# Two banded attention layers of a four-layer network: gates applied when the output is read back, projections spread over more units, modulation weights moved ahead of the output weights

## The chip, the cores and the metric

One core of a Trainium2 chip runs the whole network, 49,595 instructions in one launch. The metric is device time in microseconds (us). The kernel before was timed three times: 3087.85, 3089.04 and 3092.97 us, median 3089.04. Its engines are TensorE (PE, with its weight loads PEld), VectorE (DVE), ScalarE (ACT), GpSimd (POOL) and SyncE (SP), whose queue issues nearly all DMAs.

## The reference, cut to what matters

Four layers, each `x = x + gate * rmsnorm(mixer(h), g_post)` with `h = rmsnorm(x, g_pre) * (1 + scale) + shift`, on 1024 latent and 256 context tokens of width 1024, in float32. Scale, shift and gate are the modulation, `silu(c) @ w_ada + b_ada` with a 1024x3072 matrix for each layer. The mixers are banded attention (layers 0 and 3), latent attention (layer 1) and a chunked recurrence (layer 2). The change is in the banded layers:

```python
q_l, k_l, v_l, z_l = jnp.split(h_lat @ w_in, cuts, axis=-1)     # 1024, 256, 256 and 1024 columns
q_l = apply_rope(q_l.reshape(bsz, n_lat, A_HEADS, A_HEAD_DIM), cos, sin)   # 16 heads of 64, 4 key heads
p = sink_softmax(jnp.where(mask, logits, NEG_INF), sink_l)      # own block, its two neighbours, 256 ctx keys
o_l = jnp.moveaxis(o, 0, 1).reshape(bsz, n_lat, A_WIDTH)
y_l = (o_l * jax.nn.silu(z_l)) @ w_out
```

Layer 0 also makes queries, gates and outputs of the context tokens; layer 3 makes them for the latent tokens alone.

## The kernel before, in words

Every product is done in three matmuls, on numbers split into a high and a low part (high x high, high x low, low x high). Weights come in pieces of 512 KB: `add_chunk` and `add_mod` put pieces into one list (`todo`), `fetch` (L136) loads them in that order into three buffers (`raw`), and `step` (L151) takes the first loaded piece: a weight is split by one engine (high part) and another (low part), a modulation chunk of 256 columns, two pieces, is multiplied on PE at once (`mod_piece`, L356, and `flush_mod`, L374). `need(chunk)` steps until that chunk is there, and so also handles all that stands ahead of it in the list. `plan` (L623) sets the order of the list. In it, the next layer's twelve modulation chunks stood behind `z` chunks 2 to 7 (one each), and the other six behind the first six of the eight pieces of the output weights `wo`. Layer 3 has no next layer and no modulation.

`layer_a` (L681) first makes keys and values, then works through *units*: (key head g, tile t of 128 queries), 40 in layer 0 (two context tiles, then eight latent ones, for each g) and 32 in layer 3. Step s of the loop runs `stage_s(s)` (scores, maximum, exponential, normalization) and `stage_pv(s-1)` (transposes, `ph`/`pl` split, product with the values). PE has spare time in both, and into it `fill(n)` draws n steps of the generator `projections`, one matmul a step, which makes the queries `q` of group g (written out to `qd`) and the gates `z` (written out to `zd` with silu applied). The counts drawn are in `fs` (behind each of the four heads) and `fp` (behind each key block). Where something isn't made in time, `made_for` draws until it is. A unit before needed its queries two units ahead (`load_q`) and its two gate blocks in `stage_pv` (`load_z`, L849), where POOL multiplied the output by them (L938) ahead of the write to `od`.

At s = `last` the rest of the projections is drawn, the buffers of the projection weights and of the layer's input are given up, and `wo` takes their place: eight pieces, dealt out over the remaining units by `pacer`. At s = nu - `early` (39 of 40 in layer 0, 29 of 32 in layer 3) `boundary` (L505) begins and its matmuls become the filler. For each tile it loads the output of all heads (`go`, 512 KB, one buffer), splits it into `gh` and `gl` in halves of 512 columns (`halves`, L586), multiplies by `wo` in 48 matmuls of 512 columns, and adds the normed result to x; in layer 0 it also norms the tile for the next layer. The split of the next tile is called behind the fourth of a tile's eight rounds.

Query weights `wq` and gate weights `wz` have one buffer each, so a chunk can only be split once the chunk before it of the same kind is used up. Before, q and z pieces took turns so that one kind's split lay beside the other's matmuls.

The order written in the program isn't that of the queues: the whole program is laid out once, by a planner with a clock of its own, which can place a later instruction ahead of earlier ones of its engine when by its clock those are not yet ready. On the chip each queue then runs in the planned order.

Of the kernel before, what the change touches and what calls it, by code (L numbers as in the profile page):

```python
# [9 lines left out]
F32 = mybir.dt.float32  # L10
# [3 lines left out]
ALU = mybir.AluOpType  # L14
# [14 lines left out]
PIECES = ((0, 512), (512, 512), (1024, 256))  # L29
# [21 lines left out]
class Dit:  # L51
# [543 lines left out]

    def gload_T(self, od):

        def load(t, wk):
            o = wk.tile([128, 8, 128], F32, name="go", bufs=1)
            self.nc.sync.dma_start(out=o, in_=od[:, t * 128:t * 128 + 128].rearrange("(k p) t -> p k t", p=128))  # L600
            return o

        def split(o, wk):
            return self.halves(wk, lambda h: o[:, 4 * h:4 * h + 4, :], "act", "pool")
        return load, split
# [18 lines left out]
    def plan(self, i):  # L624
# [4 lines left out]
        P = {}  # L629
# [5 lines left out]
        if kind == "a":  # L635
            P["kv"] = self.add_chunk(w_in, 1024, 512, eo=256)
            if i == 0:
                mods(8, 12, 0)
            for g in range(4):
                P["q", g] = self.add_chunk(w_in, g * 256, 256, eo=256)  # L640
                for x in (2 * g, 2 * g + 1):
                    P["z", x] = self.add_chunk(w_in, 1536 + 128 * x, 128)
                    if x >= 2:
                        mods(x, x + 1)
            P["wo"] = [self.add_chunk(ins[f"l{i}_w_out"][x * 512:(x + 1) * 512, :], 0, 1024, 4) for x in range(2)]
            wos = [self.todo.pop() for _ in range(8)][::-1]
            rest = [x for x in list(range(4 // 2)) + list(range(8, 12))]
            for x in range(8):
                self.todo.append(wos[x])
                for m in rest[:1]:  # L650
                    mods(m, m + 1)
                rest = rest[1:]
            for m in rest:
                mods(m, m + 1)
        elif kind == "b":
# [25 lines left out]
    def layer_a(self, i, hpool, hT, hs):  # L681
# [96 lines left out]
        def proj_q(g, pieces):  # L778

            w = P["q", g]  # L780
            for t0, m in pieces:
                for b in range(2):
                    for ps in piece(w, slice(128 * b, 128 * b + 128), t0, m):
                        yield
                    if b == 0:
                        e = self.eo_even(qp, ps, t0, m)
                    else:
                        self.eo_odd(qp, e, ps, t0, m, lambda p: qd[g][p])
                made.add(("q", g, t0))

        def proj_z(x, pieces):

            w = P["z", x]
            for t0, m in pieces:
# [6 lines left out]
                nc.sync.dma_start(out=zd[x * 128:(x + 1) * 128, t0:t0 + m], in_=zs[:, 0:m])  # L801
                made.add(("z", x, t0))

        def projections():

            ctx = [PIECES[2]] if need_ctx else []
            for g in range(4):
                yield from proj_q(g, ctx + [PIECES[0]])
                yield from proj_z(2 * g, ctx + list(PIECES[:2]))
                self.need(P["z", 2 * g + 1])  # L810
                yield from proj_q(g, [PIECES[1]])
                if g < 3:
                    self.need(P["q", g + 1])
                yield from proj_z(2 * g + 1, ctx + list(PIECES[:2]))
                if g < 3:
                    self.need(P["z", 2 * g + 2])

        pq = projections()

        def made_for(kind, xs, t):  # L820

            for x in xs:
                while (kind, x, t * 128 // 512 * 512) not in made:
                    next(pq)


        fs, fp = (5, 5, 5, 2), (2, 2, 2, 2, 1)
        units = [(g, t) for g in range(4) for t in qtiles]
# [11 lines left out]
        def load_q(u):  # L840
            g, t = units[u]
            made_for("q", (g,), t)
            q = p2.tile([128, 2, 4, 128], F32R, name="qT", bufs=2)
# [4 lines left out]
            st[u] = {"qT": q}  # L848

        def load_z(u):  # L850
            g, t = units[u]
            made_for("z", (2 * g, 2 * g + 1), t)
            z = p2.tile([128, 2, 128], F32, name="zin", bufs=2)
            nc.sync.dma_start(out=z, in_=zd[g * 256:(g + 1) * 256, t * 128:(t + 1) * 128]
                              .rearrange("(a p) t -> p a t", p=128))
            st[u]["z"] = z

# [48 lines left out]
        def stage_pv(u, fill, end=False):  # L906
            g, t = units[u]
            pr, kbs = st[u]["pr"], st[u]["kbs"]
            load_z(u)
            v2 = grp[g][1]  # L910
# [25 lines left out]
            for b in range(2):  # L936
                nc.vector.tensor_tensor(out=o[64 * b:64 * b + 64], in0=pv_[:, b], in1=uv[:, b], op=ALU.add)  # L937
            nc.gpsimd.tensor_tensor(out=o, in0=o, in1=st[u]["z"], op=ALU.mult)  # L938
            nc.sync.dma_start(out=od[g * 256:(g + 1) * 256, t * 128:(t + 1) * 128]
                              .rearrange("(a p) t -> p a t", p=128), in_=o)  # L940
            del st[u]

        load_group(0)
        made_for("q", (0,), qtiles[-1])
        made_for("z", (0,), qtiles[-1])
        load_q(0)
# [10 lines left out]
        early = 3 if i == self.depth - 1 else 1  # L957
        last = nu - 7
        for s in range(nu + 1):
# [20 lines left out]
            if s == nu - early:  # L980
                for w in wo:
                    self.need(w, FAST)
                bg = self.boundary(i, wo, [gq, wop], self.gload_T(od), gq, 1 if i == self.depth - 1 else 0)
                next(bg)
# [1025 lines left out]
```

## Time and profile before

| | us |
|---|---|
| median of three runs | 3089.04 |
| the profiled execution | 3097.26 |
| its span on the core | 3095.5 |
| TensorE matmul busy in the span | 2861.1 (92%) |
| VectorE / ScalarE / GpSimd busy | 1727.5 / 1261.0 / 1288.7 |

By stretches of the span: layer 0 has its units from about 200 to 707 us, its boundary overlapping from 677 on to about 820; layer 3 has its units from about 2600 to 3040 and its boundary from 2978 to the end. A busy PE counts also the time in which it works at the lower clock, so the granted clock is read beside it.

### The profile page before, as it was taken

Reading aid. Unit: us, or ns where it says so; the run is one execution under the profiler, and the core shown is the slowest. Engines: PE = TensorE matmul, PEld = TensorE weight load, DVE = VectorE, ACT = ScalarE, POOL = GpSimd, SP = SyncE. Lnnn points to the kernel's source line nnn. Section 1 sums busy time; section 2 is a strip of 40 time slices with the busy share of each in tenths; the row PEclk is TensorE's granted clock in tenths of the full one; section 3 lists DMA queues with packets and bytes.
Section 4 is the critical chain, followed back from the end, with each engine's and each line's share of the span. In section 5 each row is a group of like instructions: output and inputs, shape, how many; then the busy total and the mean of one; then the engine's idle time right before and its main releaser. Section 6 shows DMA issues by size and latency. Waiting matters only on the chain.

```text
span 3095.5 us, 49595 instructions
## 1 busy us (share of the span) xinstructions
PE 2861.1 (92%) x17344; PEld 2478.1 (80%) x17344; DVE 1727.5 (56%) x3807; ACT 1261.0 (41%) x2665; POOL 1288.7 (42%) x1535
## 2 busy tenths in 40 slices
PE   6799999989999999999899999998887999999898
PEld 4678888768877788888787789998776788888777
DVE  3337667665522366666456644245387744666772
ACT  2226556453312355555433323132264422555552
POOL 2445555545653010100353331236475445555552
PEclk9899999999999999999999899999898999999999
DMA  7453544554354311111343343699585545434433
GB/s 236 142 151 100 176 145 125 177 159 144 97 162 160 104 44 33 34 39 31 115 144 117 123 155 121 196 310 287 199 254 201 193 130 166 123 111 137 143 91 114
DMA packets 455259, 439.85 MB, mean 142 GB/s; under 512 B 38658, under 2 KB 389146, under 8 KB 455010
## 3 DMA queue, kind: packets, MB, share of 16 engines
q1 hardware_dynamic: 448832, 426.55, 43.8%
q10 hardware_dynamic: 5746, 9.48, 1.0%
q8 instruction: 138, 2.26, 0.3%
q0 software_dynamic: 432, 0.66, 0.1%
q14 instruction: 111, 0.91, 0.1%
HBM read 301.68 MB, written 135.53 MB: 141 GB/s over the span
## 4 chain that ended last, share of the span: by engine, by line
PE 54%; DVE 11%; DMA 8%; issue 4%; ACT 3%; POOL 3%; SPq 1%; ACTq 0%; POOLq 0%; DVEq 0%
PE n L73 30%; PE w L73 18%; PE n L76 5%; DVE acc L1407 1%; DMA e<-rmd 1%; DMA raw<-in_l_w_in_dram 1%; DVE mx L1257 1%; ACT ph L81 1%; DVE cl L90 1%; POOL hl L90 1%; DVE pl L90 1%; DMA qpd<-eo_t 1%; DMA gdd<-e 1%; DVE big L426 1%; DMA raw<-in_l_w_out_dram 1%
## 5 line engine op out<-in xcount | busy, mean ns | idle before, releaser
L90 DVE TENSOR_TENSOR pl<-n,ph 128x512 fp32r<-128x512 f32 x488 | 330.0, 686 | 114.6 <-ACT ph L81 97.1
L81 ACT ACTIVATE ph<-n 128x512 fp32r<-128x512 f32 x488 | 284.4, 597 | 224.9 <-PE n L76 171.8
L73 PE MATMUL n<-ph,v 128*128 128x256 f32 (+1 forms) x992 | 292.3, 337 | 19.1 <-ACT ph L81 13.5
L76 PE MATMUL n<-ident,p 128*128 128x128 f32 x1952 | 292.6, 277 | 8.9 <-DVE o L937 3.1
L73 PE MATMUL n<-wh,hh 128*128 128x256 f32 x960 | 278.2, 290 | 15.6 <-DVE sg L1738 12.6
L895 ACT ACTIVATE p<-p,nm 128x641 f32<-128x641 f32 (+2 forms) x288 | 221.0, 769 | 155.5 <-DVE nm L893 122.0
L73 PE MATMUL n<-wl,hh 128*128 128x256 f32 x960 | 275.1, 287 | 0.0
L73 PE MATMUL n<-wh,hl 128*128 128x256 f32 x960 | 274.9, 286 | 0.0
L76 PEld LDWEIGHTS n<-ident,p 128*128 128x128 f32 x1952 | 236.6, 143 | 43.9 <-ACT p L1260 4.2
L902 POOL TENSOR_SCALAR p<-p,rl 128x640 f32<-128x640 f32 (+2 forms) x288 | 213.8, 754 | 129.2 <-DVE rl L900 95.0
L891 DVE CUSTOM_DVE_ANT_0 p<-w,mask 128x640 f32<-128x640 f32 (+2 forms) x288 | 208.2, 745 | 100.1 <-PE w L73 67.3
L73 PE MATMUL n<-pl,v 128*128 128x512 f32 (+1 forms) x656 | 237.6, 362 | 17.8 <-DVE pl L90 17.3
L1311 POOL TENSOR_TENSOR o<-o,z 128x256 f32<-128x256 f32 x40 | 30.4, 760 | 440.6 <-ACT o L1310 266.0
L73 PE MATMUL w<-ks,qT 128*128 128x256 f32 (+1 forms) x1088 | 199.5, 309 | 12.0 <-DVE mx L891 7.0
L73 PEld LDWEIGHTS n<-ph,v 128*128 128x128 f32 x992 | 175.5, 190 | 37.3 <-ACT ph L81 21.7
L73 PEld LDWEIGHTS n<-wh,hh 128*128 128x128 f32 x960 | 187.7, 196 | 19.5 <-DVE sg L1738 14.1
L73 PEld LDWEIGHTS w<-ks,qT 128*128 128x128 f32 x1088 | 176.4, 190 | 30.6 <-DVE mx L891 12.3
L73 PEld LDWEIGHTS n<-wl,hh 128*128 128x128 f32 x960 | 187.7, 196 | 0.1
L73 PEld LDWEIGHTS n<-wh,hl 128*128 128x128 f32 x960 | 187.5, 195 | 0.0
L90 POOL TENSOR_TENSOR wl<-raw,wh 128x1024 fp32r<-128x1024 f32 x38 | 96.7, 2550 | 162.7 <-DVE wh L83 161.0
L73 PEld LDWEIGHTS n<-pl,v 128*128 128x128 f32 x656 | 125.0, 191 | 35.2 <-DVE pl L90 29.4
L73 PE MATMUL n<-hh,wh 128*128 128x512 f32 (+1 forms) x336 | 125.4, 373 | 6.2 <-DVE eo_t L276 5.7
(349 smaller groups left out, 7557.1 us busy)
## 6 DMA issues: line engine op xcount, KB each, us to landing
raw<-in_l_w_ada_dram SPq DMA_DIRECT2D x96, 512.0 KB
raw<-in_l_w_in_dram SPq DMA_DIRECT2D x72, 512.0 KB
qT<-qd SPq DMA_DIRECT2D x576, 64.0 KB
raw<-in_l_w_out_dram SPq DMA_DIRECT2D x32, 512.0 KB
vd<-v SPq DMA_DIRECT2D x60, 256.0 KB
xd<-xt SPq DMA_DIRECT2D x30, 512.0 KB
od<-o SPq DMA_DIRECT2D x112, 128.0 KB
go<-od SPq DMA_DIRECT2D x28, 512.0 KB
```

The source lines that it names most:

```text
L73: self.nc.tensor.matmul(out, lhsT, rhs, start=start, stop=stop)
L76: self.nc.tensor.transpose(out, in_, self.ident)
L81: nc.scalar.activation(out=out, in_=in_, func=AF.Copy)
L90: e.tensor_tensor(out=lo, in0=src, in1=as32(hi), op=ALU.subtract)
L426: nc.vector.tensor_scalar(out=h32[:, kk, :], in0=ps[:, k * 128:(k + 1) * 128], scalar1=self.mod[i][:, 8 + kk, v:v + 1], scalar2=self.mod[i ...
L891: nc.vector.tensor_tensor_reduce(out=p[:, 0:n], in0=ps[:, s0:768], in1=mask[:, mo:mo + n], scale=1.0, scalar=-3.0e38, op0=ALU.add, op1=ALU ...
L895: nc.scalar.activation(out=p[:, 0:n + 1], in_=p[:, 0:n + 1], func=AF.Exp, scale=0.125, bias=nm[:, j:j + 1], accum_out=lsum[:, j:j + 1])
L902: nc.gpsimd.tensor_scalar(out=pr[y][:, 0:n], in0=pr[y][:, 0:n], scalar1=rl[:, y:y + 1], scalar2=0.5, op0=ALU.mult, op1=ALU.mult)
L1257: nc.vector.tensor_reduce(out=mx[:, 1:2], in_=pl, op=ALU.max, axis=AX.X)
L1311: nc.gpsimd.tensor_tensor(out=o, in0=o, in1=z, op=ALU.mult)
L1407: nc.vector.scalar_tensor_tensor(out=a, in0=xp[:, t0 + o + j:t0 + o + j + n], scalar=cw[:, j, b:b + 1], in1=a, op0=ALU.mult, op1=ALU.add)
```

## The change

In `plan`, the modulation chunks stand between the q and z chunks, one behind each from `z0` on and three behind `z6`; none stands among the output weights. The chunks of q and z change places.

```diff
-            for g in range(4):
-                P["q", g] = self.add_chunk(w_in, g * 256, 256, eo=256)
-                for x in (2 * g, 2 * g + 1):
+            for n, (kd_, x) in enumerate((("q", 0), ("z", 0), ("q", 1), ("z", 1), ("q", 2), ("z", 2), ("z", 3), ("q", 3), ("z", 4),
+                                          ("z", 5), ("z", 6), ("z", 7))):
+                if kd_ == "q":
+                    P["q", x] = self.add_chunk(w_in, x * 256, 256, eo=256)
+                else:
                     P["z", x] = self.add_chunk(w_in, 1536 + 128 * x, 128)
-                    if x >= 2:
-                        mods(x, x + 1)
+                if 0 < n < 11:
+                    mods(n - 1, n if n < 10 else 12)
...
-            for x in range(8):
-                self.todo.append(wos[x])
-                for m in rest[:1]:
-                    mods(m, m + 1)
```

The generator makes all of q0 first and runs the gates one group behind the queries; the last two gate blocks come one behind the other. More steps are drawn for each unit in layer 0, one fewer in layer 3, and `last` is later.

```diff
+            yield from proj_q(0, ctx + lat)
+            self.need(P["q", 1])
+            for g in range(1, 4):
+                yield from proj_q(g, ctx + lat[:1])
+                yield from proj_z(2 * g - 2, ctx + lat)
+                self.need(P["z", 2 * g - 1])
+                yield from proj_q(g, lat[1:])
                 if g < 3:
                     self.need(P["q", g + 1])
+                yield from proj_z(2 * g - 1, ctx + lat)
+                self.need(P["z", 2 * g])
+            yield from proj_z(6, ctx + lat)
+            self.need(P["z", 7])
+            yield from proj_z(7, ctx + lat)
...
-        fs, fp = (5, 5, 5, 2), (2, 2, 2, 2, 1)
+        fs, fp = ((6, 6, 5, 2), (2, 2, 2, 2, 2)) if need_ctx else ((5, 5, 4, 2), (2, 2, 2, 2, 1))
...
-        last = nu - 7
+        last = nu - (5 if need_ctx else 6)
```

The units no longer load or apply their gates; `boundary` loads them beside the output, one tile at a time, and POOL multiplies 1024 columns ahead of the split.

```diff
-            nc.gpsimd.tensor_tensor(out=o, in0=o, in1=st[u]["z"], op=ALU.mult)
...
+            for a, n in ((od, "go"), (zd, "gz"))[:1 if zd is None else 2]:
+                x.append(wk.tile([128, 8, 128], F32, name=n, bufs=1))
+                self.nc.sync.dma_start(out=x[-1], in_=a[:, t * 128:t * 128 + 128].rearrange("(k p) t -> p k t", p=128))
...
+            if len(x) > 1:
+                self.nc.gpsimd.tensor_tensor(out=o, in0=o, in1=x[1], op=ALU.mult)
```

## Rows read from the trace of the kernel before

**Rows 1.** The page, part 1: busy time of each engine over the span.

```profile
PE 2861.1 (92%) x17344; PEld 2478.1 (80%) x17344; DVE 1727.5 (56%) x3807; ACT 1261.0 (41%) x2665; POOL 1288.7 (42%) x1535
```

**Rows 2.** Busy time by stretch: its length, engines' busy us, PE clock, DMA share, GB/s.

```profile
200.00:250.00 50.00, 41.87 (x249) 36.07 (x249) 33.37 (x93) 24.19 (x59) 28.05 (x40) 0.97 0.43 133
250.00:590.00 340.00, 336.44 (x2023) 288.44 (x2022) 233.76 (x632) 193.45 (x418) 188.99 (x302) 1.00 0.45 136
590.00:690.00 100.00, 79.39 (x508) 61.27 (x507) 66.79 (x171) 49.02 (x99) 50.01 (x71) 0.93 0.62 194
690.00:797.00 107.00, 107.00 (x513) 89.15 (x512) 57.45 (x100) 41.62 (x67) 53.53 (x62) 1.00 0.39 131
2600.00:2640.00 40.00, 38.72 (x210) 33.04 (x209) 30.32 (x72) 19.94 (x44) 27.52 (x31) 1.00 0.44 132
2640.00:2905.00 265.00, 257.30 (x1408) 218.82 (x1407) 184.39 (x451) 148.52 (x304) 150.75 (x216) 0.99 0.42 123
2905.00:2980.00 75.00, 57.13 (x301) 47.19 (x300) 59.12 (x138) 41.56 (x87) 44.52 (x64) 0.84 0.48 138
2978.00:3088.00 110.00, 108.89 (x526) 90.42 (x524) 44.26 (x83) 39.51 (x77) 37.37 (x53) 1.00 0.32 106
```

**Rows 3.** Waits of PE, 590 to 690 us: releaser, us in total, times, longest.

```profile
PE n L73 <- DMA raw<-in_l_w_ada_dram: 9.2, 4, 4.8
PE n L73 <- ACT ph L81: 5.0, 3, 3.4
PE n L73 <- DVE pl L90: 4.4, 2, 2.3
PE w L73 <- DMA qT<-qd: 1.3, 2, 1.0
```

**Rows 4.** PE's groups of the modulation, 590 to 690 us: busy us, mean ns, idle before.

```profile
L73 PE MATMUL n<-raw,cs 128*32 128x256 f32 x112 | 10.1, 458 | 9.2 <-DMA raw<-in_l_w_ada_dram 9.2
L73 PE MATMUL n<-sel,part 128*128 128x2 f32 x32 | 5.1, 259 | 0.0
```

**Rows 5.** The same two groups of PE, 250 to 590 us.

```profile
L73 PE MATMUL n<-raw,cs 128*32 128x256 f32 x80 | 5.4, 385 | 0.0
L73 PE MATMUL n<-sel,part 128*128 128x2 f32 x16 | 2.1, 236 | 0.0
```

**Rows 6.** Waits of PE, 2905 to 2980 us.

```profile
PE n L73 <- DVE pl L90: 5.4, 4, 2.6
PE n L73 <- ACT ph L81: 4.7, 2, 3.9
PE w L73 <- DVE mx L891: 4.6, 5, 2.4
```

**Rows 7.** Waits of PE, 200 to 250 us.

```profile
PE w L73 <- DMA qT<-qd: 3.6, 1, 3.6
```

**Rows 8.** POOL's groups over the span, gate product and a two-input product of 1024 columns.

```profile
L90 POOL TENSOR_TENSOR wl<-raw,wh 128x1024 fp32r<-128x1024 f32 x38 | 96.7, 2550 | 162.7 <-DVE wh L83 161.0 <-DMA q<-qd 1.0 <-DVE mod L385 0.6
L938 POOL TENSOR_TENSOR o<-o,zin 128x256 f32<-128x256 f32 x72 | 55.2, 767 | 120.2 <-DVE o L937 108.8 <-DMA qT<-qd 5.0 <-issue 2.7
```

**Rows 9.** Timeline of one boundary tile of layer 3: start us, us, engine, instruction.

```profile
3056.03 0.37 SPq L600 DMA_DIRECT2D go<-od  x1
...
3060.16 0.63 ACT L81 ACTIVATE gh<-go 128x512 fp32r<-128x512 f32 x1 [3.33 <-DMA go<-od]
...
3060.87 1.29 POOL L90 TENSOR_TENSOR gl<-go,gh 128x512 fp32r<-128x512 f32 x1 [3.14 <-ACT gh L81]
...
3065.07 0.62 PE L73 MATMUL w<-wo0h,gh 128*128 128x512 f32 x2
...
3066.91 0.37 SPq L600 DMA_DIRECT2D go<-od  x1
```

**Rows 10.** Timelines of POOL and DVE, one moment ahead of layer 3's boundary.

```profile
2935.11 3.30 POOL L90 TENSOR_TENSOR wo1l<-raw,wo1h 128x1024 fp32r<-128x1024 f32 x1
...
2936.13 2.29 DVE L893 SCALAR_TENSOR_TENSOR nm<-mx,nsink 128x1 f32<-128x1 f32 x1
```

More of the change, by code (lines that the diff above doesn't have):

```diff
@@ L594, in halves, with gload_T, split @@
         return gh, gl
-    def gload_T(self, od):
+    def gload_T(self, od, zd=None):
         def load(t, wk):
[L599 to L603, printed above, removed]
+            x = []
+            for a, n in ((od, "go"), (zd, "gz"))[:1 if zd is None else 2]:
+                x.append(wk.tile([128, 8, 128], F32, name=n, bufs=1))
+                self.nc.sync.dma_start(out=x[-1], in_=a[:, t * 128:t * 128 + 128].rearrange("(k p) t -> p k t", p=128))
+            return x
+        def split(x, wk):
+            o = x[0]
+            if len(x) > 1:
+                self.nc.gpsimd.tensor_tensor(out=o, in0=o, in1=x[1], op=ALU.mult)
             return self.halves(wk, lambda h: o[:, 4 * h:4 * h + 4, :], "act", "pool")
@@ L788, in proj_q @@
                         self.eo_odd(qp, e, ps, t0, m, lambda p: qd[g][p])
-                made.add(("q", g, t0))
+                made.add((g, t0))
         def proj_z(x, pieces):
@@ L801, in proj_z, with made_for @@
                 nc.sync.dma_start(out=zd[x * 128:(x + 1) * 128, t0:t0 + m], in_=zs[:, 0:m])
-                made.add(("z", x, t0))
         def projections():
             ctx = [PIECES[2]] if need_ctx else []
[L807 to L811, printed above, removed]
+            lat = list(PIECES[:2])
+            yield from proj_q(0, ctx + lat)
[5 more added lines that the diff above has]
+                yield from proj_q(g, lat[1:])
                 if g < 3:
                     self.need(P["q", g + 1])
-                yield from proj_z(2 * g + 1, ctx + list(PIECES[:2]))
-                if g < 3:
-                    self.need(P["z", 2 * g + 2])
-        pq = projections()
[L820 to L824, printed above, removed]
-        fs, fp = (5, 5, 5, 2), (2, 2, 2, 2, 1)
+                yield from proj_z(2 * g - 1, ctx + lat)
[3 more added lines that the diff above has]
+            yield from proj_z(7, ctx + lat)
+        pq = projections()
+        def made_for(g, t):
+            while (g, t * 128 // 512 * 512) not in made:
+                next(pq)
+        fs, fp = ((6, 6, 5, 2), (2, 2, 2, 2, 2)) if need_ctx else ((5, 5, 4, 2), (2, 2, 2, 2, 1))
         units = [(g, t) for g in range(4) for t in qtiles]
@@ L841, in load_q @@
             g, t = units[u]
-            made_for("q", (g,), t)
+            made_for(g, t)
             q = p2.tile([128, 2, 4, 128], F32R, name="qT", bufs=2)
@@ L848, in load_q @@
             st[u] = {"qT": q}
[L850 to L856, printed above, removed]
         def cols(t):
@@ L908, in stage_pv @@
             pr, kbs = st[u]["pr"], st[u]["kbs"]
-            load_z(u)
             v2 = grp[g][1]
@@ L943, in layer_a @@
         load_group(0)
-        made_for("q", (0,), qtiles[-1])
-        made_for("z", (0,), qtiles[-1])
+        made_for(0, qtiles[-1])
         load_q(0)
@@ L982, in layer_a @@
                     self.need(w, FAST)
-                bg = self.boundary(i, wo, [gq, wop], self.gload_T(od), gq, 1 if i == self.depth - 1 else 0)
+                bg = self.boundary(i, wo, [gq, wop], self.gload_T(od, zd), gq, 1 if i == self.depth - 1 else 0)
                 next(bg)
```

5 lines of the change are left out of this document (removed).

## Prediction, made before the changed kernel was run

> **What bounds the kernel now.** I read the busy time of the engines first: TensorE works for 2861.1 of 3095.5 us and the next engine, VectorE, for 1727.5 [rows 1]. The matmuls are the same before and after, so only time in which TensorE stands still, or runs at its lower clock, can be won or lost. Second, the busy time by stretch, to see where that time lies in the two layers that the change touches [rows 2]. While projections fill the units, PE stands still for 3.6 of 340 us in layer 0 (250 to 590) and 7.7 of 265 us in layer 3 (2640 to 2905), at a clock of 1.00 and 0.99. Where the filler has run out, it stands still for 20.6 of 100 us (590 to 690, clock 0.93) and 17.9 of 75 us (2905 to 2980, clock 0.84). The beginnings lose 8.1 of 50 us in layer 0 and 1.3 of 40 us in layer 3. The boundaries lose nothing and 1.1 us. So some 39 us of idle PE and the slow clock in two stretches are what this change can reach. Third, the waits of PE in those stretches, to see what ends them: in layer 0 the largest is the load of modulation weights, 9.2 us in four waits, then the split of the probabilities (5.0 and 4.4 us) [rows 3]. In layer 3, which has no modulation, all of it is VectorE and ScalarE being late with the units' own work, 5.4, 4.7 and 4.6 us [rows 6].
>
> **The change part by part.** I sum against the profiled execution, 3097.3 us; it is 8.2 us over the median of the runs shown, and the difference found is carried to that median.
>
> *Modulation away from the output weights (layer 0).* Beside `wo`, 590 to 690 us, stand 112 matmul rows of modulation, 16 to a chunk, so seven chunks: 10.1 + 5.1 = 15.2 us of PE, 2.2 us a chunk, and 9.2 us of waiting for their weights [rows 4]. In the filled stretch five chunks (80 rows) took 5.4 + 2.1 = 7.5 us, 1.5 us a chunk, with no wait at all [rows 5]. Six of the seven move into filled units. That takes away the 9.2 us of waits and 6 x 0.7 = 4 us of slow work: 13 us. The cover at the new place is the projections and units that PE has to do meanwhile.
>
> *Two more filled units in layer 0, one in layer 3.* By the counts in the code a unit of five key blocks draws 19 + 10 = 29 steps instead of 26 in layer 0, 16 + 9 = 25 instead of 26 in layer 3. Of 1152 steps in layer 0, 217 stood ahead of the first unit and 145 do now; 22 were left over for unit 33, now 64 for unit 35. In layer 3 (768 steps) nothing was left, and now 37 are, at unit 26. The work is moved, not saved: the win is what a unit loses without filler. In layer 0 that is the waits on the splits and on queries, 5.0 + 4.4 + 1.3 = 10.7 us over the six units from 33 on [rows 3], 1.8 us each, so 3.6 us for two. In layer 3 it is 17.9 us over four units, 4.5 each, and the clock: of 57.1 busy us at 0.84 some 9 us, 2.3 a unit [rows 2]. At most 6.8 us are won there.
>
> *What is late next in layer 3.* The eight pieces of `wo` must still be split between the last projection and the boundary, now in three units' time instead of four, on the engines that PE already waits for. So I count half of the 6.8, 3 us; the ends are nothing and 6.8. In layer 0 the eight pieces lie in fewer units too, but without twelve modulation pieces between them; I take 1 us lost, between nothing and the 9.4 us of both split waits.
>
> *New waits for weights.* Queries and gates no longer take turns everywhere. q1's weights can be split only behind q0's last matmul, and q1 is the first filler now, where z1 was. The same holds for z6 and z7, each needed right behind the gate block before it, and in layer 0 three modulation chunks and z7, seven pieces of 512 KB through three buffers, are called for together. Queued behind such a wait on PE are the units' scores; the planner can put units ahead of it, and the queue of SP can load early. The trace has no such wait in a filled stretch. Below, the price is nothing, as for the five chunks in rows 5; above, it is the same 9.2 us of modulation loads once more [rows 3] and, at each layer's start, a second wait like the 3.6 us for queries [rows 7]: 16 us in all. A loss only, since nothing is taken off PE here. I take 4 us in layer 0, 2 at the start of layer 3.
>
> *Gates in the boundary.* POOL gives up 72 products of 0.77 us and gets 18, of ten and eight tiles, of the size of a two-input product that takes 2.55 us [rows 8]: 55 us go, 46 come, none of it on PE. SP loses 72 loads and gets 18. What counts is the chain of a tile in layer 3 [rows 9]: the load is issued at 3056.03, the high split starts at 3060.16 and the low one ends at 3062.16; the tile's matmuls begin at 3065.07. With 2.55 us put between load and split, the high part ends at 3060.16 + 2.55 + 0.63 = 3063.3 and the low part at 3064.7, both ahead of the matmuls. So it is hidden, with 1.7 us over for the high part and about 1.3 us for the low one, which is used behind two pairs of matmuls (0.62 us a pair, overlapping). The gates' load goes behind the output's on the same queue. If it lands within 1.3 us of it, or is issued earlier (its buffer comes free earlier), nothing is lost; if it takes a second 4.13 us, 2.9 us are lost in each tile. The DMA engines are at 0.32 and 0.39 there [rows 2], so I stay near the lower end: 1 us, between nothing and 18 x 2.9 = 52 us.
>
> Where POOL's products cost something is VectorE: the tiny 128x1 `nm` of a unit, took 2.29 us from 2936.13 and ended at 2938.42, and POOL's two-input product, begun before it, ended at 2938.41 [rows 10]. In layer 3 six tiles or so (62 us of units beside the boundary, 2978 to 3040, by 10.9 us a tile [rows 9]) will have the 2.55 us product beside units that still run, so VectorE may be held for up to 6 x 2.55 = 15 us. PE has boundary matmuls to do then, so I add nothing. The Trainium skill, "SBUF — State Buffer", section "Who interferes with whom", says that the two engines share a pair of ports as a lock: an instruction of VectorE with two inputs in that memory stands still until GpSimd's is through. The trace agrees in that row. By the rule the hold comes with every product that meets an `nm`, so I leave it 0.02 of the slower side.
>
> **The sum.** Layer 0: -13 - 3.6 + 1 + 4 = -11.6. Layer 3: -3 + 2 = -1. Boundaries +1. Together -11.6, of which I take -11: 3097.3 - 11 = 3086.3 in a profile like this one, 3089.0 - 11 = 3078 us for the median.
>
> **The rivals.**
>
> *The waits travel along.* The modulation loads are late again where three chunks and z7 come together (9.2 us), and both starts lose 3.6 us: -11.6 + (9.2 + 7.2 - 6) = -1, so 3088 us. For it: single buffers, and a queue that can't leave its planned order when a load takes longer than planned. Against: five chunks in filled units without a wait.
>
> *The boundary is gated by its loads: slower.* Output and gates, 1 MB a tile, land one after the other, and the product and the splits run late, 2.9 us in each of 18 tiles, at worst +52. It decides once the second load lands more than 1.3 us behind the first. At half of it, 1.5 us a tile, the sum is -11 + 26 = +15, so 3104 us. For it: one buffer each, and the next load is issued only when the tile's last low split is done (3066.91, behind 3065.59 + its duration). Against: DMA engines two thirds idle, and the gates' buffer is free 4 us before the output's.
>
> *All of the tail is filled.* PE loses nothing from the split waits or the clock either: layer 0's 20.6 us of idle and some 6 of clock, half of layer 3's 27: about -27 + 4 waits for weights, so 3066 us. Against: 64 and 37 steps are drawn in a lump and not dealt out, and three or four units in each layer still have no filler.
>
> *The planner undoes it.* Since it can pull later work forward already, fewer forced draws may leave its order as good as it was: 0, 3089 us. It shares its place with the first rival.
>
> **How the numbers follow.** A change of less than 0.2%, 6.2 us, can't be told from none here. The forecast, -6 to -18, gets 0.46; the full tail, -18 to -30, 0.14; the waits that travel and the planner, between -6 and +6, 0.26; the boundary, or a start that costs more than both tails give, over +6, 0.12, with the 0.02 for held units 0.14. So faster 0.60, same 0.26, slower 0.14. The range goes from the full tail, 3063, to the upper part of no change, 3094; outside are the gated boundary and the last of the tail, 0.18.
>
> **What would show it.** Right: 590 to 690 without a wait for the modulation load; PE idle in layer 0's last units cut from 20.6 to near 10 us and the clock near 1.00; layer 3 idle for about 15 us ahead of its boundary; the boundary's PE as full as before, with the product ending some 2 us ahead of the tile's first matmul. Wrong: waits of PE for modulation or for `wz` near the last gate blocks, more than 12 us of idle at the start of layer 0, or gaps on PE ahead of each boundary tile with the gates' load as the releaser.

## The result, and the profile after

The changed kernel takes 3107.2 us (median of four runs, 3106.71 to 3107.87), where the kernel before took 3088.8 beside it: 1.0057 times as long, 95% interval 1.004 to 1.0075. It is 18 us slower. The forecast was 3078 us, 3063 to 3094, and slower had 0.14.

The profiled execution of the changed kernel is 3106.71 us, at its median; that of the kernel before was 8 us above its own. So the two profiles differ by 9.4 us only, and a stage read from one pair of them is good to some microseconds. First the page's first part, to be held against [rows 1]:

```profile
PE 2860.1 (92%) x17344; PEld 2472.4 (80%) x17344; DVE 1737.2 (56%) x3807; ACT 1261.6 (41%) x2665; POOL 1288.0 (41%) x1481
```

The work is as large as before, and POOL has its 54 instructions less. Next the stretches that answer to those of [rows 2]: 682 to 821 us is layer 0's boundary, and layer 3's tail is read 9 us later, as it begins later here (length, then busy us of PE, PEld, DVE, ACT, POOL, PE's clock, DMA share, GB/s):

```profile
250.00:590.00 340.00, 331.34 (x2021) 281.43 (x2021) 231.65 (x630) 189.50 (x409) 161.18 (x263) 0.99 0.44 132
590.00:690.00 100.00, 80.50 (x446) 65.02 (x445) 62.74 (x148) 43.73 (x90) 52.15 (x63) 0.88 0.52 159
682.00:821.00 139.00, 130.28 (x605) 105.93 (x603) 68.58 (x117) 48.99 (x82) 81.20 (x76) 0.98 0.41 129
2640.00:2905.00 265.00, 258.71 (x1427) 219.86 (x1426) 184.71 (x462) 150.04 (x306) 136.63 (x199) 1.00 0.38 112
2914.00:2989.00 75.00, 62.62 (x317) 51.25 (x317) 55.61 (x125) 38.02 (x79) 44.47 (x56) 0.91 0.53 153
```

PE stands still for 8.7 us in layer 0's filled units (before 3.6), for 19.5 us between 590 and 690 at a clock of 0.88 (before 20.6 at 0.93), and for 8.7 us in a boundary in which [rows 2] show none up to 797 us. Only layer 3's tail has gained: 12.4 us still, at 0.91 (before 17.9 at 0.84).

To place the time I cut each profile at the same events: from the first matmul of layer 0's query projection to the first `wo` matmul ("units 0"), from there to the first projection of layer 1 ("boundary 0"), from there to the first query projection of layer 3 ("layers 1, 2"), and to layer 3's first `wo` matmul ("units 3"). What follows, layer 3's boundary up to the last write of the output, is 95 us in every kernel below. Each ratio is to runs of the kernel before from the same round; their median is 3088.8 to 3091.8 us, so medians of different rounds can be compared to some 3 us only. Labels with a_ start from the changed kernel, those with b_ from the one before, those with due_ from b_mods_gates_due.

| kernel | median us | ratio to before, 95% interval | units 0 | boundary 0 | layers 1, 2 | units 3 |
|---|---|---|---|---|---|---|
| before | 3088.8 | 1 | 522.0 | 126.5 | 1762.6 | 429.9 |
| after | 3107.2 | 1.0057 (1.004 to 1.0075) | 528.5 | 138.7 | 1762.4 | 422.9 |
| a_mods_even | 3101.4 | 1.0033 (1.002 to 1.0046) | 527.7 | 135.5 | 1771.5 | 425.6 |
| a_nogate | 3085.0 | 0.9972 (0.996 to 0.9984) | 522.8 | 127.1 | 1762.7 | 421.1 |
| a_dve | 3108.2 | 1.0052 (1.0032 to 1.0071) | 529.1 | 135.1 | 1761.3 | 424.9 |
| b_gates | 3108.7 | 1.0053 (1.0038 to 1.0068) | 531.7 | 137.0 | 1761.9 | 424.0 |
| b_mods | 3068.2 | 0.9922 (0.99 to 0.9944) | 501.2 | 127.1 | 1752.6 | 427.1 |
| b_mods_gates | 3094.3 | 1.0008 (0.9994 to 1.0022) | 512.0 | 138.9 | 1763.8 | 424.7 |
| b_mods_gates_due | 3078.1 | 0.9963 (0.995 to 0.9976) | 502.0 | 141.0 | 1752.8 | 423.0 |
| b_mods_gates_two | 3090.1 | 1.0004 (0.9994 to 1.0013) | 510.4 | 135.2 | 1766.3 | 426.1 |
| due_load_only | 3068.8 | 0.9928 (0.9913 to 0.9943) | 503.9 | 127.1 | 1759.4 | 427.3 |
| due_product_only | 3090.8 | 1.0003 (0.9992 to 1.0014) | 505.3 | 133.8 | 1776.5 | 424.7 |
| due_two_dve | 3084.9 | 0.9983 (0.9969 to 0.9996) | 508.1 | 132.2 | 1755.4 | 430.1 |
| b_mods_g3 | 3070.0 | 0.9927 (0.991 to 0.9945) | 502.0 | 127.1 | 1758.1 | 425.6 |
| b_mods_counts | 3080.7 | 0.9972 (0.9957 to 0.9986) | 513.1 | 126.7 | 1758.2 | 425.1 |
| b_mods_last | 3077.5 | 0.9963 (0.9949 to 0.9976) | 501.0 | 128.8 | 1764.4 | 428.6 |
| b_mods_draws | 3075.6 | 0.9955 (0.994 to 0.9969) | 507.2 | 127.5 | 1758.4 | 421.9 |

So after lost 6.5 us in units 0 and 12.2 in boundary 0, and won 7.0 in units 3. In units 0 as a whole PE stands still as long as before (32.7 us, before 32.3): the loss is longer busy time, at a granted clock of 0.96 instead of 0.98. In boundary 0, 6.6 of the 12.2 us are idle time (8.7 us, before 2.1), the rest busy time (clock 0.98, before 1.00).

Layers 1 and 2 have the same source in all but three of them (due_product_only, and the two kernels with two buffers, see below), but not the same planned order, and their length lies between 1752.6 and 1771.5 us in the profiles of the others: no verdict below rests on that column. One execution is also not the median. The profiled one of a_mods_even is 13 us above its kernel's median; those of the others are within 6 us of theirs, but for that of the kernel before.

What PE waits for in the changed kernel, 600 to 700 us (releaser, us in total, times, longest):

```profile
PE n L73 <- DVE pl L90: 7.4, 2, 4.1
PE n L73 <- DMA raw<-in_l_w_ada_dram: 6.3, 2, 5.9
PE n L73 <- ACT ph L81: 1.5, 2, 1.2
PE n L73 <- DVE wzh L83: 1.3, 1, 1.3
```

and in its boundary, 690 to 820 us:

```profile
PE w L73 <- POOL gl L90: 6.4, 4, 2.1
PE w L73 <- ACT gh L81: 0.9, 1, 0.9
```

Of the three signs named for "wrong", the first is there: PE waits for a modulation load, as in [rows 3], now at the batch of three chunks, and for `wz` behind it. The second isn't: from 154 to 250 us PE is still for 4.6 us, not over 12. The third is half there: gaps ahead of the boundary's matmuls, but the releaser is the low split behind the product and not the gates' load.

### The profile page after: what moved, and what is told of

It reads as the page before. It is cut to its first block, busy times and chain, and to the rows that moved or that the text cites. A ratio compares the mean times of both kernels' runs of the same rounds, so it can differ in the third digit from the quotient of the medians.

```text
span 3104.9 us, 49425 instructions
## 1 busy us (share of the span) xinstructions
PE 2860.1 (92%) x17344; PEld 2472.4 (80%) x17344; DVE 1737.2 (56%) x3807; ACT 1261.6 (41%) x2665; POOL 1288.0 (41%) x1481
## 5 line engine op out<-in xcount | busy, mean ns | idle before, releaser
L73 PEld LDWEIGHTS n<-wh,hh 128*128 128x128 f32 x960 | 187.1, 195 | 20.6 <-DVE sg L1728 14.5
## 6 DMA issues: line engine op xcount, KB each, us to landing
raw<-in_l_w_ada_dram SPq DMA_DIRECT2D x96, 512.0 KB
raw<-in_l_w_in_dram SPq DMA_DIRECT2D x72, 512.0 KB
raw<-in_l_w_out_dram SPq DMA_DIRECT2D x32, 512.0 KB
xd<-xt SPq DMA_DIRECT2D x30, 512.0 KB
go<-od SPq DMA_DIRECT2D x28, 512.0 KB
```

The costliest lines, as they stand in the source:

```text
L73: self.nc.tensor.matmul(out, lhsT, rhs, start=start, stop=stop)
```

## The experiments

**The batch of three modulation chunks.** In the changed kernel, chunks are dealt out so that none stands right ahead of `z7`.

```diff
-                if 0 < n < 11:
-                    mods(n - 1, n if n < 10 else 12)
+                mods(*((0, 0), (0, 1), (1, 2), (2, 3), (3, 5), (5, 6), (6, 7), (7, 9), (9, 10), (10, 12), (0, 0), (0, 0))[n])
```

> The changed kernel with the three modulation chunks behind z6 moved up to z2, q3 and z5, so that none stands between z6 and z7. Theory: the loss in layer 0's units is the wait of TensorE for modulation weights where three chunks are called together; then the stretch around 600 to 615 us has no such wait, the units end 8 to 10 us sooner and the time is 3097 to 3100 us. Rival: it is the dealing itself (64 steps in a lump, the output weights split in fewer units); then the wait goes, another takes its place and the time stays at 3107 us within 3.

It gave 3101.4 us, between the two; its interval and that of after just overlap. The load wait has gone, but units 0 are 527.7 us in its profile, 0.8 less than in the changed kernel. Waits of PE, 600 to 700 us:

```profile
PE n L73 <- DVE pl L90: 8.1, 3, 4.0
PE w L73 <- DVE mx L883: 2.3, 2, 2.1
PE n L73 <- ACT ph L81: 1.6, 1, 1.6
```

So this wait was real, but not the main cause: the units' own splits stand behind it and take its place. What taking it away is worth, between nothing and the 6 us of the medians, stays open, since the profiled execution is 13 us above its median.

**The gates in the boundary, from both sides.** a_nogate is the changed kernel without the gates' load and product (its result is without the gates):

```diff
-                bg = self.boundary(i, wo, [gq, wop], self.gload_T(od, zd), gq, 1 if i == self.depth - 1 else 0)
+                bg = self.boundary(i, wo, [gq, wop], self.gload_T(od), gq, 1 if i == self.depth - 1 else 0)
```

> The changed kernel without the gates in the boundary: neither loaded nor multiplied, so the gates are left out of the result. Theory: the load and the product in the chain of each tile cost layer 0's boundary its 12 us; then that boundary is 116 to 117 us long as before, layer 3's stays, and the time is 3094 to 3097 us. Rival: the boundary is late for what came before it (output weights, the next layer's weights); then it stays near 128 us and the time near 3107 us.

It takes 3085.0 us, 22 less than after (26 by the ratios), more than the theory gave; boundary 0 is back at 127.1, 11.6 us shorter, and units 0 are 5.7 shorter. With the gates left out, the rest of the change is 0.28% faster than the kernel before, some 9 us.

b_gates is the kernel before with the gates moved and nothing else:

```diff
-    def gload_T(self, od):
+    def gload_T(self, od, zd=None):
...
-            load_z(u)
...
-            nc.gpsimd.tensor_tensor(out=o, in0=o, in1=st[u]["z"], op=ALU.mult)
```

> The kernel before with this part alone: gates multiplied in the boundary, none in the units; list, generator and counts as before. Theory: it loses the 12 us of the boundary and wins little in the units (72 loads and products fewer, some 2 us): 3097 to 3101 us. Rival: the product only hurts beside the later tail; then 3087 to 3090 us.

It takes 3108.7 us, as slow as the whole change: both theories had too little. Boundary 0 grows by 10.5 us, and units 0 by 9.7, which neither foresaw. The modulation loads, still beside `wo` here, are later than before (in total, times, longest, 560 to 700 us; [rows 3] has 9.2):

```profile
PE n L73 <- DMA raw<-in_l_w_ada_dram: 15.9, 3, 8.7
```

**The modulation alone.** The kernel before, with all twelve chunks behind the gate chunks and none beside `wo`:

```diff
-                    if x >= 2:
-                        mods(x, x + 1)
+                    mods(*((0, 1), (1, 2), (2, 4), (4, 5), (5, 7), (7, 8), (8, 10), (10, 12))[x])
...
-            wos = [self.todo.pop() for _ in range(8)][::-1]
...
```

> The kernel before with this part alone: the six modulation chunks that stood among the output weights stand behind z chunks, one or two at each, none among the output weights. Theory: as predicted for this part, waits of 9.2 us and some 4 us of slow work go: 3076 to 3081 us. Rival: the waits only move to other places, since the tail's time is set by the splits of the output weights: 3086 to 3090 us.

3068.2 us, 24 less than before beside it (3091.8), and better than the theory. It is the fastest kernel run. Busy times of the kernel before from 154 to 250 us, then of b_mods from 154 to 250, 250 to 570 and 570 to 670 us, and below them the waits of PE in b_mods from 560 to 680:

```profile
154.00:250.00 96.00, 86.49 (x467) 74.47 (x468) 42.30 (x107) 29.26 (x69) 48.14 (x53) 0.94 0.50 147
```

```profile
154.00:250.00 96.00, 95.45 (x558) 82.38 (x558) 46.24 (x126) 33.30 (x79) 52.57 (x62) 0.97 0.59 174
250.00:570.00 320.00, 316.96 (x1949) 269.76 (x1948) 216.99 (x596) 179.55 (x390) 176.34 (x276) 1.00 0.49 145
570.00:670.00 100.00, 87.22 (x501) 72.17 (x501) 74.04 (x186) 57.09 (x119) 61.24 (x88) 0.95 0.52 163
```

```profile
PE n L73 <- ACT ph L81: 6.8, 4, 2.3
PE n L73 <- DVE pl L90: 3.3, 2, 2.2
PE w L73 <- DVE mx L881: 2.3, 2, 1.5
```

No load is left among the waits (9.2 us before), and in the start, 154 to 250 us, PE stands still for 0.6 us, before for 9.5. Over the whole of units 0 it stands still for 16.1 us instead of 32.3, and its busy time is 4.6 us shorter: together the 20.8 us that units 0 are shorter. The split waits are as large as in [rows 3].

**Gates on top of it.** b_mods_gates joins the two.

> The kernel before with two parts: modulation among the z chunks and gates multiplied in the boundary of both layers; order, counts and last unit as before. Theory: the parts add up, modulation alone gave -24 us and gates alone +17 us, so 3083 to 3088 us, with layer 0's boundary 137 us long, and what the changed kernel lacks against this one, some 20 us, is due to the new order of the projections and its counts. Rival: the two parts get in each other's way and this is as slow as the changed kernel, 3100 to 3108 us; then order and counts cost nothing.

3094.3 us: the gates cost 26 us on this base, eleven in units 0 and twelve in boundary 0, and eat the whole gain. Both theories placed it wrongly, the median in between. Busy times, 250 to 570 us, to be held against the second line above:

```profile
250.00:570.00 320.00, 312.04 (x1917) 264.07 (x1915) 224.68 (x616) 185.78 (x404) 154.22 (x259) 1.00 0.43 129
```

PE is still for 8.0 us in the filled units, not 3.0. The code says why this could be: `load_z` also *drew* the gate projections. Without its demand the draws that it forced (30, 40 and 40 steps, counted in the code) are left for the lump at s = `last`, 132 steps instead of 22.

b_mods_gates_due puts the demand back without the load:

```diff
             pr, kbs = st[u]["pr"], st[u]["kbs"]
+            made_for("z", (2 * g, 2 * g + 1), t)
```

> Modulation among the z chunks and gates in the boundary, with order and counts of before, and z still drawn when a unit of before would have needed it (the draw alone, no load). Theory: taking the gates out of the units took away the draws that kept the projections in time (30, 40 and 40 steps in layer 0), so that 132 steps instead of 22 were left for the lump at unit 33; with the draws back layer 0's units are 501 to 505 us long as with modulation alone, not 512, and the time is 3080 to 3087 us. Rival: the units are longer because the first tiles of the boundary wait for gates and product; then 510 to 514 us and 3090 to 3097 us.

3078.1 us, 16 less (14 by the ratios) and 2 below the range expected, and units 0 are 502.0, as expected (unit 31 ends 434 us after the first query matmul and unit 32 12 us later; in b_mods_gates 416, and 40 later). So the lost draws are the 10 us that units 0 lost there; the boundary, 141.0, is untouched by them. The rest of the 16 stands in layers 1 and 2 of the profiles (1763.8 against 1752.8 us), whose source is the same. And the 132 steps are this kernel's: the changed kernel, with its higher counts, has 64 left.

**What of the boundary?** Three kernels changed the product's place or its buffers. a_dve multiplies on VectorE (`nc.vector` for `nc.gpsimd`, on the changed kernel):

> The changed kernel with the gate product of the boundary on VectorE instead of GpSimd. Theory: in layer 0's boundary GpSimd is in the chain of a tile with four pieces of work (product 2.4, two low splits 2.6, the next layer's low part 2.4 us), and the low part of the tile comes late by 1.5 to 2.5 us; VectorE needs about 1.2 us for the product, so the waits of TensorE for gl (6.4 us) go and that boundary is 127 to 131 us long instead of 139: 3097 to 3101 us. Rival: the second load is what is late; then the boundary stays near 138 us and the time at 3105 to 3109 us.

3108.2 us, no gain, as the rival had it; the boundary 135.1, not 127 to 131. POOL's low split hardly holds PE there any more, but other things do, `wlat`, layer 1's first weights, at the boundary's end (waits of PE, 690 to 820 us):

```profile
PE n L73 <- ACT wlath L81: 4.0, 1, 4.0
PE w L73 <- ACT gh L81: 2.4, 2, 1.3
PE w L73 <- POOL gl L90: 0.6, 3, 0.2
```

b_mods_gates_two gives the loads two buffers (`bufs=2`, on b_mods_gates):

> Modulation among the z chunks and gates in the boundary, with order and counts of before, and two buffers each for the output and gate tiles that the boundary loads. Theory: the boundary of layer 0 loses its 12 us because the load waits for the last low split and the product then falls together with the other splits on GpSimd; with the load a tile ahead the product can lie early, and the boundary is 127 to 130 us long instead of 139: 3082 to 3087 us. Rival: GpSimd's work in a tile is what is too much whatever the load does; then it stays at 136 us or more and the time at 3091 to 3097 us.

3090.1 us and 135.2: it takes back a third of the boundary's loss, and is in neither theory's range. (This edit, and with it due_two_dve, gives layer 1's boundary two buffers as well.) Then, on b_mods_gates_due, the load without the product (the result is without the gates), the product without the load, and both remedies together:

```diff
-            if len(x) > 1:
-                self.nc.gpsimd.tensor_tensor(out=o, in0=o, in1=x[1], op=ALU.mult)
```

> The kernel with the modulation among the gate chunks, the gates in the boundary and the units' draws for gates kept, but with the gates loaded for each boundary tile and no product taken (the result is without the gates). Theory: layer 0's boundary is late by the product on POOL and by what is planned around it, so without it the stretch from the first output matmul to the first layer-1 projection goes from 141.0 back to 126-129 us, and the median to 3063-3070. Rival: the 512 KB of gates behind the 512 KB of output on one queue are what is late; the stretch stays at 137-142 us and the median at 3075-3081.

```diff
-            for a, n in ((od, "go"), (zd, "gz"))[:1 if zd is None else 2]:
+            for a, n in ((od, "go"), (zd, "gz"))[:1]:
...
-            if len(x) > 1:
-                self.nc.gpsimd.tensor_tensor(out=o, in0=o, in1=x[1], op=ALU.mult)
+            self.nc.gpsimd.tensor_tensor(out=o, in0=o, in1=o, op=ALU.mult)
```

> The same kernel with the product but no load of gates: each boundary tile's output is multiplied by itself, so the gates are left out and the result is another. Theory (the product): layer 0's boundary stays at 136-142 us, the median at 3074-3081. Rival (the load): 126-129 us, and 3063-3070. If both this and the kernel with the load alone lie between, near 133 us, the two share the cost.

```diff
-                x.append(wk.tile([128, 8, 128], F32, name=n, bufs=1))
+                x.append(wk.tile([128, 8, 128], F32, name=n, bufs=2))
...
-                self.nc.gpsimd.tensor_tensor(out=o, in0=o, in1=x[1], op=ALU.mult)
+                self.nc.vector.tensor_tensor(out=o, in0=o, in1=x[1], op=ALU.mult)
```

> The same kernel with gates loaded and multiplied, two buffers for each load, and the product on VectorE, so that the load can run a tile ahead and POOL has only the splits. Theory (the chain of load and product in one buffer, on an engine that also makes the next layer's low splits): with both taken away the boundary of layer 0 is back at 126-130 us, the median at 3064-3071. Rival: it is the work itself, on whichever engine, beside the next layer's norm: 133-139 us, and 3074-3081.

The load alone is free: 127.1 us and 3068.8, as b_mods with no gates in its boundary. So it is the product: 9.3 us in the medians (3078.1 - 3068.8), and 13.9 in the boundary of the profiles. With the product alone the boundary is 133.8, between the two; its 1.89 us is a shorter product than the real one's 2.40. This edit does more than it was meant to: it multiplies in every boundary that reads its output back this way, layer 1's too, so in 28 tiles and not 18:

```profile
L607 POOL TENSOR_TENSOR go<-go x28: 1892/1893/2865, 588.9 to 3067.8; 128x1024 f32<-128x1024 f32 x28
```

The output matmuls of layer 1's boundary, which take 128.9 to 131.8 us in every other kernel, take 138.0 there. So its median, 3090.8, can't be held against that of the kernel with both; but these ten products, in a layer without gates, show the product's cost a second time. With both remedies layer 0's boundary is still 132.2, and the median, 3084.9, is 7 us worse than without them. Of the 5.1 us by which that boundary is longer than with the load alone, 2.0 are PE's waits for `gl` and 2.2 a longer wait for layer 1's first weights at its end (4.3 for 2.1).

Where the product sits can be read off one tile of the changed kernel (timelines of SP, POOL and PE, start us, us):

```profile
741.32 0.37 SPq L602 DMA_DIRECT2D go<-od  x1
749.28 0.37 SPq L602 DMA_DIRECT2D gz<-zd  x1
...
754.48 0.36 SPq L602 DMA_DIRECT2D go<-od  x1
```

```profile
746.87 2.39 POOL L608 TENSOR_TENSOR go<-go,gz 128x1024 f32<-128x1024 f32 x1 [3.52 <-DMA go<-od]
749.21 2.39 POOL L90 TENSOR_TENSOR hl<-big,hh 128x1024 fp32r<-128x1024 f32 x1
751.54 1.28 POOL L90 TENSOR_TENSOR gl<-go,gh 128x512 fp32r<-128x512 f32 x1
752.90 0.19 POOL L96 TENSOR_SCALAR ms<-ss 128x1 f32<-128x1 f32 x1
753.17 1.28 POOL L90 TENSOR_TENSOR gl<-go,gh 128x512 fp32r<-128x512 f32 x1
```

```profile
749.97 0.73 PE L73 MATMUL w<-wo0h,gh 128*128 128x512 f32 x2 [0.93 <-ACT gh L81]
...
752.87 0.96 PE L73 MATMUL w<-wo0h,gl 128*128 128x512 f32 x2 [1.71 <-POOL gl L90]
```

The product ends 0.7 us ahead of the tile's first matmul, and still PE waits: `hl` stands between the product and the low half. `go` has one buffer, so this is a loop: issue, landing 5.5 us later, product, the next layer's low split `hl`, two halves of `gl`, next issue. It takes 754.48 - 741.32 = 13.2 us here, and 13.8 to 14.6 in the three that follow. In the kernel before the same loop, at the same place, is kept by PE at

```profile
744.06 0.37 SPq L600 DMA_DIRECT2D go<-od  x1
...
755.81 0.37 SPq L600 DMA_DIRECT2D go<-od  x1
```

11.75 us a tile, and so it is with the load alone:

```profile
736.14 0.37 SPq L602 DMA_DIRECT2D go<-od  x1
747.92 0.37 SPq L602 DMA_DIRECT2D go<-od  x1
```

Over the last six tiles PE takes 70.6 us before and with the load alone, 81.1 after, 76.3 with the short product: 10.5 of the 12.2 us. In layer 3, where no `hl` stands in the loop, the changed kernel's tile goes

```profile
3054.67 0.36 SPq L602 DMA_DIRECT2D go<-od  x1
...
3065.56 0.36 SPq L602 DMA_DIRECT2D go<-od  x1
```

10.89 us, PE's own pace in [rows 9] (3066.91 - 3056.03 = 10.88): there it just fits.

Two buffers don't open this loop, as b_mods_gates_two's trace shows (timelines of SP and POOL):

```profile
722.66 0.37 SPq L602 DMA_DIRECT2D go<-od  x1
...
736.35 0.37 SPq L602 DMA_DIRECT2D go<-od  x1
```

```profile
728.15 2.40 POOL L608 TENSOR_TENSOR go<-go,gz 128x1024 f32<-128x1024 f32 x1 [3.48 <-DMA go<-od]
730.51 1.29 POOL L90 TENSOR_TENSOR gl<-go,gh 128x512 fp32r<-128x512 f32 x1
731.76 2.39 POOL L90 TENSOR_TENSOR hl<-big,hh 128x1024 fp32r<-128x1024 f32 x1
735.03 1.29 POOL L90 TENSOR_TENSOR gl<-go,gh 128x512 fp32r<-128x512 f32 x1
```

The load is a tile ahead now, but so is the product in POOL's order: it stands ahead of the `gl` of the tile before it. That tile's `gh` ended at 725.64, and its `gl` starts only at 730.51, behind a product that had to wait for its own load. The next load waits for the second `gl`, and so it is 13.7 us from issue to issue again. That the loop sets PE's pace is read from these tiles; no run changed POOL's order alone.

**Gates moved in layer 3 alone**, on b_mods:

```diff
-            load_z(u)
+            if need_ctx:
+                load_z(u)
...
-                bg = self.boundary(i, wo, [gq, wop], self.gload_T(od), gq, 1 if i == self.depth - 1 else 0)
+                bg = self.boundary(i, wo, [gq, wop], self.gload_T(od, None if need_ctx else zd), gq, 1 if i == self.depth - 1 else 0)
```

> The kernel before with modulation among the z chunks, and gates multiplied in the boundary in layer 3 alone. Theory: layer 3 has no next layer's norm in its boundary and its tile chain has time left (its boundary was 95.0 us long with and without gates), while its units won 6 us without gate loads and products: 3060 to 3064 us, the fastest so far. Rival: the 6 us of layer 3 came with the changed layer 0 by chance of the planned order: 3067 to 3070 us.

3070.0 us against 3068.2, and 425.6 against 427.1 in units 3: neither gain nor loss, as the rival had it.

**The draws and the later end.** On b_mods, the two edits together, then each alone:

```diff
-        fs, fp = (5, 5, 5, 2), (2, 2, 2, 2, 1)
+        fs, fp = ((6, 6, 5, 2), (2, 2, 2, 2, 2)) if need_ctx else ((5, 5, 4, 2), (2, 2, 2, 2, 1))
...
-        last = nu - 7
+        last = nu - (5 if need_ctx else 6)
```

> The kernel before with two parts: modulation among the z chunks, and the changed kernel's counts of steps and its later last unit; order of the projections as before, gates in the units. Theory: the counts are harmless or a small gain (two more filled units, -4 us), and it is the order of queries and gates, with split and use of one buffer back to back, that costs the changed kernel 20 us: 3063 to 3071 us. Rival: the later last unit costs it, since the output weights are split in five and four units instead of seven and five: 3080 to 3090 us.

> Modulation among the z chunks, with the changed kernel's later last unit (nu - 5 and nu - 6 instead of nu - 7) and the counts of before. Theory: the later last unit alone costs layer 0 its 12 us, since the eight pieces of the output weights must be split in five units instead of seven where VectorE is already late: units 511 to 515 us, 3078 to 3083 us. Rival: the higher counts cost it; then 500 to 504 us and 3066 to 3071 us.

> Modulation among the z chunks, with the changed kernel's counts of steps and the last unit of before. Theory: higher counts only move draws and cost nothing: layer 0's units 499 to 504 us, 3065 to 3071 us. Rival: they take the time from the units' own chain and cost the 12 us: 511 to 515 us and 3078 to 3083 us.

Together they cost 12.5 us (3080.7 against 3068.2; 15 by the ratios), and units 0 grow by 11.9: the theory, that they help a little, fell. But they don't fill two more units here. With the old order of the projections, 217 steps stand ahead of the first unit, and by the counts in the code all 1152 are drawn by unit 33 as in b_mods: the last projection ends 72.0 us ahead of the first `wo` matmul, 68.8 in b_mods. In the changed kernel it is 49.4, before 85.9. So these three kernels show what higher counts and a later end cost without more filler. Which of the two it is isn't settled. The later end alone costs 9 us in the median, though units 0 are 501.0 in its profile; the draws alone cost 7, with units 0 at 507.2. Intervals overlap. With both, the splits of the last units are waited for longer than in b_mods (waits of PE, 560 to 680 us):

```profile
PE w L73 <- DVE mx L881: 5.5, 5, 4.0
PE n L73 <- DVE pl L90: 4.6, 4, 1.7
PE n L76 <- DVE o L927: 1.9, 1, 1.9
```

**Do the parts add up?** By the ratios: modulation -0.78%, gates +0.86% on top of it (1.0008 - 0.9922), counts +0.50% (0.9972 - 0.9922), together +0.58%; the whole change measures +0.57%. That they meet shows less than it seems to: the gates' part holds the draws lost with 132 steps left over, and the counts' part two units that aren't filled, and neither is so in the changed kernel. What can be said of the changed kernel itself comes from a_nogate: gates in the boundary +0.85% (1.0057 - 0.9972), all the rest -0.28%. How that rest divides among modulation, draws, new order, later end and the batch of three wasn't run.

## Why the prediction was wrong

**Modulation, -13 us: right, and too small.** On the kernel before it is -24 in the medians, -20.8 in units 0. The 9.2 us of loads went as worked out. What the sum lacked is the start, where PE stands still for 9.0 us less (0.6 for 9.5); why the moved chunks help there isn't shown. I had read the start's wait for queries [rows 7] only as a thing that could be doubled.

**"Hidden, with 1.7 us over", boundary +1 us: this step failed.** On the changed kernel itself the gates in the boundary cost 22 us (3107.2 against 3085.0), 11.6 of them in boundary 0; that is nearly the whole miss. It is the product and not the load, as the kernels on b_mods_gates_due show. The tile I worked it from [rows 9] is one of layer 3, and for layer 3 it holds. Layer 0's ten tiles also norm the next layer's input, and POOL's `hl`, 2.39 us, stands between the product and `gl`. And I asked whether the product ends ahead of the tile's matmuls, which it does, instead of how long the loop from load to load becomes: 13.2 us and more, where PE has 11.8 to hide it. The rival "gated by its loads" described that loop and has nearly the right time (3104), but for a cause that isn't one: the second load costs nothing (3068.8 against 3068.2).

**The gates' demand: counted, but at no price.** `load_z` forced draws. The 64 steps that the prediction has left over are right for a kernel without it, but it put nothing in the sum for drawing them in a lump. On b_mods, with 132 left, the lost draws cost 10 us in units 0 (16 in the medians, 3094.3 against 3078.1). What the 64 cost in the changed kernel no run shows. Little of the miss can be due to them, since all the rest of the change, with this lump in it, makes the kernel 4 to 9 us faster.

**Two more filled units, -3.6 us, and `wo` in fewer of them, +1 us: not seen, and not tested by themselves.** The stretch without filler became 36.5 us shorter (49.4 for 85.9), but PE is idle for 19.5 us between 590 and 690 (20.6 before), at a clock of 0.88 instead of 0.93, and units 0 aren't shorter. On b_mods the higher counts and the later end cost 12.5 us, with no unit more filled: near the upper bound for `wo`, 9.4 us, of which I took 1.

**Weight waits, +4 us in layer 0: right where they were put, wrong in what they cost.** The batch waits 6.3 us for its load and 1.3 for `wz`, as the first rival had it. Taking it away shortens units 0 by 0.8 us in the profiles, since the splits wait in its place, and the median by 6. The start, for which 3.6 us were feared, is no worse: from 154 to 250 us PE is still for 4.6 us, before for 9.5.

**Layer 3, -1 us.** Its units are 7.0 us shorter in the profile, but moving the gates there changes no time that can be measured, and the counts in layer 3 alone were not run. Whether those 7 us are the change's or the execution's stays open.

The miss in numbers, each good to some 5 us: -11 was forecast and +18 measured. Of the 29 us between, 21 to 25 are the gates in the boundary (22 by the medians, 26 by the ratios, for 1). Everything else together came to between -4 and -9 us, with -12 forecast. That this is near is luck: modulation alone, on the kernel before, gives twice what the sum has for it, and the other parts take most of it back.

One rival was added up wrongly: in "All of the tail is filled" the three parts make 40 us and not 27, so by its own terms it would be 3053 us.

## What to carry to other kernels

Work out what is hidden as a loop, from a buffer's load to its next load, with all that the engine does in between and in the order of its queue, and do it in every stage that runs the code: the one where it just fits (10.9 of 10.9 us) says nothing of the one with a third user. When an operation is removed, look for what its demand ordered ahead of it; keep the demand if you move the work. And time the parts alone: here one of them is worth 24 us, and the others take it all back. A part timed on another base can hold something that the whole doesn't, so take parts away from the changed kernel as well.

## What the runs showed of the hardware

The product of 128x1024 takes 2.40 us on POOL and 1.23 on VectorE (medians of 18), but one of VectorE's took 3.09, beside a low split on POOL, and POOL's next split of 512 columns took 2.25 instead of 1.30. In the kernel with two buffers and the product on VectorE (timelines of DVE and POOL):

```profile
724.09 3.09 DVE L608 TENSOR_TENSOR go<-go,gz 128x1024 f32<-128x1024 f32 x1 [0.37 <-issue]
```

```profile
723.70 2.40 POOL L90 TENSOR_TENSOR hl<-big,hh 128x1024 fp32r<-128x1024 f32 x1 [1.66 <-ACT hh L81]
726.06 2.25 POOL L90 TENSOR_TENSOR gl<-go,gh 128x512 fp32r<-128x512 f32 x1
...
729.18 1.30 POOL L90 TENSOR_TENSOR gl<-go,gh 128x512 fp32r<-128x512 f32 x1
```

So a product on the faster engine can still hold up POOL's splits, and they it: of a_dve's 18 products three took over 2.5 us. The Trainium skill, "SBUF — State Buffer", section "Who interferes with whom", says that these two engines have one pair of ports in common, which only one of them holds at a time; the trace agrees, 3.09 us for 1.23.

A tile multiplied by itself on POOL took 1.89 us (median of 28, due_product_only) where two tiles took 2.40.
